# The second feed-forward product by Strassen's scheme, in a transformer layer on one Trainium2 core

## The chip, the cores and the metric

The kernel runs on one core of one Trainium2 chip. The metric is the device time of one execution in microseconds (us); the figure shown for a kernel is the median of several runs. All times below are in us unless another unit stands beside them. Engines: PE is the matrix engine, DVE the vector engine, ACT the scalar engine, POOL the GpSimd engine, and SP the engine on whose queue nearly all DMAs are issued here.

## The reference

One layer of a transformer, with T = 1024 tokens, D = 1024, 16 heads of 64, and a feed-forward width of 2816, in float32:

```
shift1, scale1, gate1, shift2, scale2, gate2 = split(silu(c) @ ada_w + ada_b)
h = x * (1 + scale1) + shift1
y = forgetting_attention(h)                # q, k rms-normed; scores + F_q - F_k, causal softmax; * sigmoid(o); @ w_o
x = layer_norm(ALPHA * x + gate1 * y, ln_g[0], ln_b[0])
h = x * (1 + scale2) + shift2
gate, up = split(h @ ffn_w_in)             # (1024 x 1024) @ (1024 x 5632): the first product
u = silu(gate) * up
out = layer_norm(ALPHA * x + gate2 * (u @ ffn_w_out), ln_g[1], ln_b[1])   # (1024 x 2816) @ (2816 x 1024): the second product
```

Accuracy needs more than one pass of PE: each operand is split into a high and a low part (`hi` is the operand cast to the type fp32r by ACT, `lo` the difference made by DVE), and each product is three matmuls, hi*hi + hi*lo + lo*hi.

## The kernel before, in words

The program is written as Python loops, and a framework puts the instructions of all engines in their final order before the kernel runs; each engine then works through its own list in that order. So the order on an engine can differ from the order of the source, and it is fixed at run time: an instruction that has to wait holds up what stands behind it on its engine or queue.

Stages, with their stretch in the profile: the conditioning and the projections to q, k, v (0 to about 341); the attention (about 341 to 655); the attention's output projection (to about 780); the first feed-forward product (to about 1209); the second, with the last layer norm (to the end).

**Attention.** Head by head. `load` brings a head's operands from DRAM (qa, ka, qb, kb, va). `scores` makes the scores of tiles j = 4, 5, 6, 7, then 0 with 1 and 2 with 3, each in one of two PSUM buffers (`bankS`, tag S, bufs=2), and runs the softmax on each: DVE adds the mask on the diagonal block (L540) and takes the row maximum (L542), ACT exponentiates out of PSUM (L543). A buffer is free again when its exponentials are done. `values` transposes the probabilities on PE (L596), ACT and DVE split them (`ph` L601, `pl` L602), and PE multiplies them with va (L579, L580). `gates` makes the output gate's product (`og`, L631), 24 matmuls for each half of a pair of heads, which can stand anywhere and fill PE. The main loop (L709) takes 12 steps per head, and in each runs a few `og` matmuls, a piece of the next head's scores, and a piece of this head's values. The gate's tanh is followed on POOL by a scaling (L636) and the gate is applied on POOL (L657, L659).

**First product.** Already by Strassen's scheme in Winograd's form: 7 products of half size instead of 8, for 22 blocks of 128 hidden units. `step` runs one product of 12 matmuls into PSUM and combines it on DVE; POOL makes the sums of weights and the product with silu; `prepare` splits the weights eight products ahead. `store_hidden` splits the hidden values (ACT L963, DVE L964) and spills both parts to DRAM (`us`).

**Second product.** Plain: hidden blocks in groups of two (the last has four), eight token tiles, for each 6 matmuls of 512 columns per hidden block (L170 to L172). After each group DVE adds the PSUM tile to a sum in SBUF (L1159). `split_wout` makes ready the weights: POOL multiplies a 128x1024 block by gate2 (L992), ACT casts (L1000), DVE subtracts (L1001). `rest_of_rows` adds the residual rows, three POOL operations of 128x1024 per token tile (L1098 to L1100). With the last group the layer norm of each token tile follows on DVE (L1153, L1154, L1169), its inverse root on POOL (L751).

```
for step in range(12):
    ...
    run(gg, GC[h % 2][step])
    if nxt:
        run(nxt[2])
    run(v)
```

Of the kernel before, what the change touches and what calls it, by code (L numbers as in the profile page):

```python
# [16 lines left out]
P = 128  # L17
# [28 lines left out]
def fox_trunk_kernel(  # L46
# [469 lines left out]

    yp = ctx.enter_context(tc.tile_pool(name="yp", bufs=1, side="right", reuse_waits="tile"))
# [191 lines left out]
    for h in range(H):  # L709
# [3 lines left out]
        for step in range(12):  # L713
            if h % 2 and step in (1, 5):
                hf = HALVES[step == 5]
                state[pr][1][hf] = inverse_sums(pr, hf, state[pr][0][hf])
            if h == H - 1:
                if step == 1:
                    open_h2(HB, hTp, (f"h{HA}", f"l{HA}"))
                    yh, yl = h2h[HB], h2l[HB]  # L720
                if 2 <= step < 2 + NP - 1:
                    split_y(HA, step - 2, yh, yl, nc.gpsimd)
                if step == 6:
                    wo_first = wo_weights(HA, 0, ((ld[0], "owr", 1), (ld[0], "va", 1)))
            run(gg, GC[h % 2][step])
            if nxt:
                run(nxt[2])
            run(v)
# [30 lines left out]
    g2d = dram.tile([1, D], F32, name="g2d")  # L759
    nc.sync.dma_start(g2d, gate2b[0:1, :])  # L760
# [74 lines left out]
    def prepare(n):  # L835
# [11 lines left out]
        if n >= n_first and i == ORDER[-1]:  # L847
            if ff + 2 < NF:
                load_raw(ff + 2)
            else:  # L850
                for m in range(2):
                    load_wraw(ff % 2 * 2 + m)

    wraws = {}

    def load_wraw(ff):
        t = wraws[ff] = ld[0].tile([P, D], F32, name=f"wq{ff}r", tag=RAWS[ff % 4],
                                   **({"bufs": 1} if ff % 4 == 1 else {}))
        nc.sync.dma_start(t, fwo[ff * P:(ff + 1) * P, :])
# [68 lines left out]
    def second_half(k):  # L928
# [9 lines left out]
        hb, hb4 = [fp.tile([P, 512], F32, name=f"hb{n}_{k}", tag=f"hb{n}", bufs=2 - n) for n in range(2)]  # L938
# [3 lines left out]
        t2 = fp.tile([P, 512], F32, name=f"t2_{k}", tag="t2")  # L942
# [17 lines left out]
    def store_hidden(ff, hf, t):  # L960
# [4 lines left out]
        for j, s in enumerate((hi, lo)):  # L965
            move(nc, us[ff][j, :, hf * 512:(hf + 1) * 512], s)


    RING = 6
    rings, parts = {}, {}  # L970

    def load_u(ff):

        r = (ff + 1) % RING
        if r < 4:
            for j in range(2):
                if j not in rings:
                    rings[j] = h2p.tile([P, 4, 2, 512], F32R, name=f"ur{j}", tag="hl"[j])
            t = [rings[j][:, r] for j in range(2)]
        else:  # L980
            if 2 not in rings:
                rings[2] = hTp.tile([P, 2, 2, 2, 512], F32R, name="ur2", tag=f"h{HB}")
            t = [rings[2][:, r - 4, j] for j in range(2)]
        for j in range(2):
            move(nc, t[j].rearrange("p a b -> p (a b)"), us[ff][j])
        parts[ff] = [t, None]

    def split_wout(ff):

        r = (ff + 1) % RING  # L990
        raw = wraws[ff]
        nc.gpsimd.tensor_tensor(raw, raw, gate2b, ALU.mult)  # L992
        if r < 4:
            t = opened[0][:, 2 * r:2 * r + 2]
        else:
            if 3 not in rings:
                rings[3] = Xp.tile([P, 2, 2, 2, 512], F32R, name="wr2", tag="B22")
            t = rings[3][:, r - 4]
        raw2 = raw.rearrange("p (c e) -> p c e", c=2)
        nc.scalar.copy(t[:, :, 0, :], raw2)  # L1000
        nc.vector.tensor_tensor(t[:, :, 1, :], raw2, f32(t[:, :, 0, :]), ALU.subtract)  # L1001
        parts[ff][1] = t

    def ahead(n):
        if n == 0:
            nc.sync.dma_start(gate2b, g2d.to_broadcast([P, D]))
        elif n == 3:
            for ff in range(2):
                load_u(ff)
                split_wout(ff)  # L1010
        elif n == 5:
            load_u(2)
            split_wout(2)

    late = []

    def step(n):
# [30 lines left out]
        elif i == 4:  # L1048
# [3 lines left out]
            late.append(lambda: store_hidden(ff, HA, ua))  # L1052
        else:
# [3 lines left out]
            late.append(lambda: store_hidden(ff, HB, ub))  # L1057
# [31 lines left out]
    accs3 = {hf: hTp.tile([P, 4, D], F32, name=f"out{hf}", tag=f"{t}{HA}") for hf, t in ((HA, "h"), (HB, "l"))}  # L1089
    def out_row(tt):  # L1090
        return accs3[tt // 4][:, tt % 4, :]

    def rest_of_rows(tts):

        for tt in tts:
            t = Xp.tile([P, D], F32, name=f"x1{tt}", tag=f"T{(1, 4)[tt % 2]}")
            nc.sync.dma_start(t, x1d[tt])
            nc.gpsimd.tensor_tensor(t, t, gbs[0], ALU.mult)  # L1098
            nc.gpsimd.tensor_tensor(t, t, gbs[1], ALU.add)
            nc.gpsimd.tensor_tensor(out_row(tt), out_row(tt), t, ALU.add)  # L1100

    groups = [2] * 9 + [4]

    def load_group(n):
        g0 = sum(groups[:n])
        for ff in range(g0, g0 + groups[n]):
            if ff not in parts:
                load_u(ff)
            if ff not in wraws:
                load_wraw(ff)  # L1110
            if parts[ff][1] is None:
                split_wout(ff)

    load_group(1)
    gbs = []
    for n, src in enumerate((ln_g, ln_b)):
        gb = fp.tile([P, D], F32, name=f"gb{n}", tag=f"gb{n}")
        nc.sync.dma_start(gb, src[0, 0:1].to_broadcast([P, D]))
        nc.scalar.mul(gb, gb, ALPHA)
        gbs.append(gb)  # L1120
    tiles = [hf * 4 + o for hf in HALVES for o in range(4)]
    g0 = 0
    for gi, G in enumerate(groups):
        last = gi == len(groups) - 1
        if last:
            lnr = []
            for n, src in enumerate((ln_g, ln_b)):
                t = fp.tile([P, D], F32, name=f"ln2_{n}", tag=f"gb{n}")
                nc.sync.dma_start(t, src[0, 1:2].to_broadcast([P, D]))
                lnr.append(t)  # L1130
        for ti, tt in enumerate(tiles):
            hf, o = divmod(tt, 4)
            end = last and tt == tiles[-1]
            cuts = [(0, 512), (512, 768), (768, 896), (896, 1024)] if end else [(0, 512), (512, 1024)]
            st = fp.tile([P, 4, 6], F32, name=f"st2_{tt}", tag="st2", bufs=2) if last else None
            a = out_row(tt)
            if last and o % 2:
                ys = [ps2.tile([P, 512], F32, name=f"y{g0}_{tt}{cc}", tag="gu"[cc % 2], bufs=2)[:, 0:c1 - c0]
                      for cc, (c0, c1) in enumerate(cuts)]
            else:  # L1140
                y = bankS(f"y{g0}_{tt}").rearrange("p a b -> p (a b)")
                ys = [y[:, c0:c1] for c0, c1 in cuts]
# [65 lines left out]
```

## Time and profile before

| what | value |
|---|---|
| median of 3 runs (lowest, highest) | 1475.2 (1474.42, 1475.4) |
| the profiled execution: its time, its span | 1476.91, 1475.1 |
| busy: PE, DVE, ACT, POOL | 95%, 66%, 38%, 32% of the span |
| mean granted clock of PE | 0.987 of full speed |

PE is busy nearly all the time. A share of 95% is an average over stages: how much a stage leaves idle, and what PE waits for there, has to be read stage by stage. Below, a matmul's duration overlaps the next one's, so the rate of PE is read from the distance between starts.

### The profile page before, as it was taken

To read this page: it belongs to the slowest core of one execution; us is meant where nothing else is said; L and a number is where in the kernel's file an instruction comes from. 1 tells how busy PE (TensorE), PEld (TensorE's weight loads), DVE (VectorE), ACT (ScalarE), POOL (GpSimd) and SP (SyncE) were. 2 spreads that over 40 slices of the span, in tenths; PEclk is the share of its full clock that TensorE was granted. 3 is DMA by queue.
4 is the path that set the end of the run, shared out by engine and by line. 5 is a ranking of instruction groups with operands and counts; after the bars stand their busy time and mean duration, and the time that the engine had idled before them with its cause. 6 is when DMAs were issued, how large, how long until landed. Compare 5 with 4: busy or idle time off the path is not lost.

```text
span 1475.1 us, 19125 instructions
## 1 busy us (share of the span) xinstructions
PE 1396.3 (95%) x6955; PEld 1159.3 (79%) x6955; DVE 968.2 (66%) x1526; ACT 554.0 (38%) x1018; POOL 476.3 (32%) x312
## 2 busy tenths in 40 slices
PE   5899999999999999999998989999999998999997
PEld 4677778877888888889986767888888777777886
DVE  6766576546888888887678655454444554656568
ACT  3432232225777777772445333333333332101000
POOL 2442013300111111140035544444444427784102
PEclk9999999999999999999999999999999999999999
DMA  9757776567656666456363334333333257464212
GB/s 275 198 169 244 231 214 193 172 210 169 142 136 143 146 146 145 116 172 201 128 184 87 129 129 129 105 110 101 114 103 111 101 203 268 143 225 162 73 68 100
DMA packets 194880, 228.45 MB, mean 155 GB/s; under 512 B 11417, under 2 KB 136673, under 8 KB 194786
## 3 DMA queue, kind: packets, MB, share of 16 engines
q1 hardware_dynamic: 193634, 225.13, 50.5%
q10 hardware_dynamic: 1152, 2.10, 0.4%
q8 instruction: 55, 0.90, 0.3%
q14 instruction: 39, 0.32, 0.1%
HBM read 167.88 MB, written 59.31 MB: 154 GB/s over the span
## 4 chain that ended last, share of the span: by engine, by line
PE 63%; DVE 17%; POOL 6%; DMA 5%; issue 4%; ACT 3%; SPq 1%; POOLq 0%; DVEq 0%; ACTq 0%
PE og L631 5%; PE y L170 4%; PE y L171 4%; PE y L172 4%; PE t L596 4%; PE B L1029 3%; PE B L1030 3%; PE B L1031 3%; PE A L1029 3%; PE A L1030 2%; PE A L1031 2%; PE s L535 2%; PE s L536 2%; PE D L1031 2%; PE D L1030 2%
## 5 line engine op out<-in xcount | busy, mean ns | idle before, releaser
L1159 DVE TENSOR_TENSOR out<-y,out 128x1024 f32<-128x1024 f32 x64 | 77.8, 1221 | 79.4 <-PE y L172 77.9
L602 DVE TENSOR_TENSOR pl<-t,ph 128x512 fp32r<-128x512 f32 x192 | 103.7, 548 | 14.9 <-ACT ph L601 13.4
L1029 PE MATMUL B<-XT,slots 128*128 128x512 f32 x264 | 104.2, 395 | 7.0 <-DVE fd L1045 5.3
L543 ACT ACTIVATE p<-s,nm 128x640 f32<-128x640 f32 (+7 forms) x128 | 95.4, 746 | 39.0 <-DVE nm L542 38.6
L601 ACT CAST ph<-t 128x512 fp32r<-128x512 f32 x192 | 90.8, 478 | 44.4 <-PE t L596 42.0
L1030 PE MATMUL B<-XT,slots 128*128 128x512 f32 x264 | 103.1, 390 | 0.0
L1031 PE MATMUL B<-XT,slots 128*128 128x512 f32 x264 | 102.9, 390 | 0.0
L170 PE MATMUL y<-slots,ur 128*128 128x512 f32 (+1 forms) x246 | 96.0, 390 | 6.8 <-DVE out L1159 6.5
L542 DVE TENSOR_REDUCE nm<-s 128x1 f32<-128x640 f32 (+7 forms) x128 | 95.5, 748 | 2.5
L596 PE MATMUL t<-ident,p 128*128 128x128 f32 x576 | 95.6, 274 | 0.6 <-DVE pl L602 0.4
L171 PE MATMUL y<-slots,ur 128*128 128x512 f32 (+1 forms) x246 | 95.3, 387 | 0.0
L172 PE MATMUL y<-slots,ur 128*128 128x512 f32 (+1 forms) x246 | 95.2, 387 | 0.0
L964 DVE TENSOR_TENSOR ul<-fd,uh 128x512 fp32r<-128x512 f32 x44 | 37.5, 851 | 87.8 <-ACT uh L963 87.8
L1029 PE MATMUL A<-h2h,slots 128*128 128x512 f32 x176 | 73.5, 418 | 14.2 <-ACT fc L1039 6.7
L596 PEld LDWEIGHTS t<-ident,p 128*128 128x128 f32 x576 | 71.3, 141 | 11.5 <-DVE pl L602 2.3
L845 ACT CAST slots<-wi 128x512 fp32r<-128x512 f32 x88 | 54.0, 618 | 61.7 <-PE D L1030 35.6
L846 DVE TENSOR_TENSOR slots<-wi,slots 128x512 fp32r<-128x512 f32 x88 | 73.9, 840 | 4.5 <-ACT slots L845 4.1
L579 PE MATMUL o<-ph,va 128*128 128x512 f32 x192 | 76.6, 399 | 0.0
L535 PE MATMUL s<-ka,qa 128*128 128x320 f32 (+2 forms) x192 | 67.5, 352 | 4.8 <-ACT p L543 4.8
L1031 PE MATMUL A<-h2h,slots 128*128 128x512 f32 x176 | 71.3, 405 | 0.0
L1030 PE MATMUL A<-h2l,slots 128*128 128x512 f32 x176 | 71.1, 404 | 0.0
L580 PE MATMUL o<-pl,va 128*128 128x512 f32 x192 | 66.7, 348 | 0.0
(620 smaller groups left out, 3981.2 us busy)
## 6 DMA issues: line engine op xcount, KB each, us to landing
wi<-in_ffn_w_in_dram SPq DMA_DIRECT2D x50, 512.0 KB
aw<-in_ada_w_dram SPq DMA_DIRECT2D x46, 512.0 KB
ur<-us SPq DMA_DIRECT2D x44, 512.0 KB
us<-uh SPq DMA_DIRECT2D x44, 256.0 KB
us<-ul SPq DMA_DIRECT2D x44, 256.0 KB
qa<-qs SPq DMA_DIRECT2D x32, 256.0 KB
vs<-vt SPq DMA_DIRECT2D x16, 512.0 KB
ka<-ks SPq DMA_DIRECT2D x32, 256.0 KB
```

The lines of the kernel that those rows point to most:

```text
L170: nc.tensor.matmul(acc, lh, rh, start=(k == 0), stop=False)
L171: nc.tensor.matmul(acc, lh, rl, start=False, stop=False)
L172: nc.tensor.matmul(acc, ll, rh, start=False, stop=(k == kn - 1))
L535: nc.tensor.matmul(o, qa[:, q], ka[:, c0:c0 + w], start=True, stop=False)
L542: nc.vector.tensor_reduce(nm, view, axis=axis, op=ALU.max, negate=True)
L543: nc.scalar.activation(pv, view, AF.Exp, bias=nm, accum_out=lcs[hf][:, s * 4 + jj:s * 4 + jj + 1])
L596: nc.tensor.transpose(tb[:, jj * P:(jj + 1) * P], probs[hf * 4 + jj][:, kbk * P:(kbk + 1) * P], ident)
L601: nc.scalar.copy(ph[:, c0:], tb[:, c0:])
L602: nc.vector.tensor_tensor(pl[:, c0:], tb[:, c0:], f32(ph[:, c0:]), ALU.subtract)
L1029: nc.tensor.matmul(b, hi, rh, start=(first and k == 0), stop=False, skip_group_check=True)
L1030: nc.tensor.matmul(b, hi, rl, start=False, stop=False, skip_group_check=True)
L1031: nc.tensor.matmul(b, lo, rh, start=False, stop=(k == 3), skip_group_check=True)
```

## The change

The second product becomes Strassen's scheme too: 7 chains over 11 pairs of hidden blocks, each step 4 row tiles x 3 matmuls of 512 columns, the whole chain kept in PSUM: 7 x 11 x 12 = 924 matmuls of 512 columns, where before there were 22 x 8 x 2 x 3 = 1056 (each counted as 512 columns wide). Its operands are sums of quarters of the hidden matrix and of `ffn_w_out`:

- The sums of the weights are made during the attention, one pair of hidden blocks with each of heads 1 to 11 (`out_weights`): two 512 KB loads into the tiles `gate1b` and `gate2b`, four POOL subtractions of 128x512, two 512 KB stores to DRAM (`td`). The two gates themselves are kept in DRAM meanwhile (`gd`) and loaded again later.
- The sums of the hidden values are made by DVE at the end of each pair in the first product, four additions of 128x512 (`hidden_sums`), and stored unsplit; the ACT cast and the DVE subtraction of `store_hidden` are gone.
- The residual rows are scaled in the first product, on DVE (`scaled_row`: two operations of 128x1024 for each of 8 rows), not on POOL in the second.
- In the second product `prep2` splits each of the 77 operand pairs of 128x1024 (ACT, DVE); gate2 is applied to the result on DVE, by a multiplication and an addition of 128x512 per quarter; POOL keeps only the inverse roots.

```diff
+    def out_weights(j, step):
+        b11, b12 = gate1b[:, 0:512], gate1b[:, 512:1024]
+        b21, b22 = gate2b[:, 0:512], gate2b[:, 512:1024]
+        if step == 1:
+            for n, t in enumerate((gate1b, gate2b)):
+                nc.sync.dma_start(t, fwo[(2 * j + n) * P:(2 * j + n + 1) * P, :])
+        elif 4 < step < 9:
+            o, a, b = ((b11, b12, b11), (b12, b22, b12), (b22, b22, b11), (b21, b21, b22))[step - 5]
+            nc.gpsimd.tensor_tensor(o, a, b, ALU.subtract)
+        elif step == 11:
+            for n, t in enumerate((gate1b, gate2b)):
+                nc.sync.dma_start(td[j][:, n].rearrange("p c e -> p (c e)"), t)
...
+            if 1 <= h <= NJ:
+                out_weights(h - 1, step)
...
-        hi = fp.tile([P, 512], F32R, name=f"uh{ff}{hf}", tag="hb0", bufs=2)
-        lo = fp.tile([P, 512], F32R, name=f"ul{ff}{hf}", tag=f"a{hf}")
-        nc.scalar.copy(hi, t)
-        nc.vector.tensor_tensor(lo, t, f32(hi), ALU.subtract)
+    def hidden_sums(ff, ua, ub, va, vb):
...
+        nc.vector.tensor_tensor(s1, ub, vb, ALU.add)
+        nc.vector.tensor_tensor(s2, s1, ua, ALU.subtract)
+        nc.vector.tensor_tensor(ub, ua, ub, ALU.subtract)
+        nc.vector.tensor_tensor(s4, va, s2, ALU.subtract)
...
+        elif i == 7:
+            nc.vector.tensor_tensor(rw[0], rw[0], gate1b, ALU.mult)
+        elif i == 5:
+            nc.vector.tensor_tensor(rw[0], rw[0], gate2b, ALU.add)
...
-        nc.gpsimd.tensor_tensor(raw, raw, gate2b, ALU.mult)
...
+    def prep2(m):
...
+        nc.scalar.copy(t[:, 0], raw)
+        nc.vector.tensor_tensor(t[:, 1], raw, f32(t[:, 0]), ALU.subtract)
...
+    def add_gated(tt, c, t, src):
+        a = rows2[:, tt, c * 512:(c + 1) * 512]
+        todo.append(lambda: nc.vector.tensor_tensor(t, src, gate2b[:, c * 512:(c + 1) * 512], ALU.mult))
+        todo.append(lambda: nc.vector.tensor_tensor(a, a, t, ALU.add))
...
+        if i != ORDER2[-1]:
+            for j in range(NJ):
+                for r in range(4):
+                    products(bs[r], m0 + j, r, 0, 512, NJ)
+                    if j == NJ - 1:
+                        done(i, r, bs[r])
+                if j < NJ - 2:
+                    prep_next(m0 + j + 14, 2)
...
+        for r in range(4):
...
+            for k, (c0, c1) in enumerate(cuts):
+                for j in range(NJ):
+                    products(bs[r], m0 + j, r, c0, c1, NJ)
...
+                if k == 0 and r < 2:
+                    second_rows(2 * r)
+                    second_rows(2 * r + 1)
+                last_rows(r, bs[r], c0, c1, st, k)
```

The framework's final order moves with it, in the attention above all. The first place is PE at the start of head 9's scores. A row gives the source line, the operation, out<-in and the shape; `s9_4` is head 9's score tile 4, `t8` are transposes for the values of head 8, `o7` a values product of head 7, `og4` a gate product. Before, these rows follow one another:

```order
L535 MATMUL s9_4_4927<-ka9_4907,qa9_4906 128x320
L536 MATMUL s9_4_4927<-kb9_4909,qb9_4908 128x320
L596 MATMUL t8_1_0_4931<-ident_58,p8_4_4655 128x128
L596 MATMUL t8_1_0_4931<-ident_58,p8_5_4705 128x128
L596 MATMUL t8_1_0_4931<-ident_58,p8_6_4741 128x128
L596 MATMUL t8_1_0_4931<-ident_58,p8_7_4786 128x128
L579 MATMUL o7_0_4901<-ph7_0_2_4876,va7_4398 128x256
L580 MATMUL o7_0_4901<-pl7_0_2_4877,va7_4398 128x256
L631 MATMUL og4_1_4924<-hTl1_114,woh40_4833 128x512
L535 MATMUL s9_4_4927<-ka9_4907,qa9_4906 128x320
L536 MATMUL s9_4_4927<-kb9_4909,qb9_4908 128x320
```

And of the change, at the same tile (L556 and L557 are the score matmuls there, L617 the transposes, L601 a values product):

```order
L601 MATMUL o8_0_5224<-pl8_0_3_5221,va8_4707 128x128
L557 MATMUL s9_4_4998<-kb9_4980,qb9_4979 128x320
L556 MATMUL s9_4_4998<-ka9_4978,qa9_4977 128x320
L557 MATMUL s9_4_4998<-kb9_4980,qb9_4979 128x320
L557 MATMUL s9_5_5041<-kb9_4980,qb9_4979 128x384
L556 MATMUL s9_5_5041<-ka9_4978,qa9_4977 128x384
L557 MATMUL s9_5_5041<-kb9_4980,qb9_4979 128x384
L556 MATMUL s9_6_5078<-ka9_4978,qa9_4977 128x448
L557 MATMUL s9_6_5078<-kb9_4980,qb9_4979 128x448
L556 MATMUL s9_6_5078<-ka9_4978,qa9_4977 128x448
L557 MATMUL s9_6_5078<-kb9_4980,qb9_4979 128x448
L617 MATMUL t9_1_0_5249<-ident_58,p9_4_4999 128x128
```

The scores of head 9 no longer stand spread among the values of head 8: all values of head 8 stand ahead of them, and between score tiles 6, 7, 0 and 2 stands one transpose of head 9 itself. Heads 5, 7, 11 and 13 look the same. With heads 6, 8, 10 and 12 the scores are bunched likewise, but some rows of the head before and of the gate (2 to 4 of each kind) stand between tiles 5 and 7. Heads 0 to 4, 14 and 15 stand nearly as before, and so do the output projection and the first product.

The second place is SP's queue where the operands of head 8 are loaded. Before:

```order
L42 DMA qa8_4640<-qs4_121 64x1024
L42 DMA ka8_4641<-ks4_129 64x1024
L42 DMA qa8_4640<-qs4_121 64x1024
L42 DMA va7_4398<-vs0_133 128x8x128
L42 DMA ka8_4641<-ks4_129 64x1024
L42 DMA qb8_4642<-qs4_121 64x1024
L42 DMA qb8_4642<-fq_135 4x1024
L42 DMA kb8_4643<-ks4_129 64x1024
```

And of the change (`td5` are the stores of the sums of pair 5, which wait for POOL; `gate1b` and `gate2b` now hold blocks of `ffn_w_out`):

```order
L529 DMA gate2b_107<-in_ffn_w_out_dram 128x1024
L42 DMA qa8_4703<-qs4_121 64x1024
L42 DMA ka8_4704<-ks4_129 64x1024
L535 DMA td5_2783<-gate1b_106 128x1024
L535 DMA td5_2783<-gate2b_107 128x1024
L42 DMA qa8_4703<-qs4_121 64x1024
L42 DMA ka8_4704<-ks4_129 64x1024
L42 DMA qb8_4705<-qs4_121 64x1024
L42 DMA qb8_4705<-fq_135 4x1024
L42 DMA kb8_4706<-ks4_129 64x1024
L42 DMA kb8_4706<-fk_136 4x1024
L42 DMA va8_4707<-vs1_134 128x8x128
```

Most of head 8's operands, qb8 and kb8 among them, now stand behind two stores that wait for four POOL subtractions, which in turn stand on POOL's list behind a gate's scaling.

## Rows read from the trace of the kernel before

**Rows 1.** Busy us and instructions by stretch, PE, PEld, DVE, ACT, POOL; granted clock; DMA.

```profile
1209.00:1300.00 91.00, 82.52 (x348) 66.57 (x347) 48.25 (x32) 20.48 (x22) 65.90 (x26) 0.96 0.57 208
1425.00:1475.00 50.00, 42.27 (x205) 35.60 (x203) 42.01 (x70) 0.00 (x0) 11.37 (x8) 0.93 0.22 85
```

**Rows 2.** PE in time after a stall, start and duration; then the stretch behind it.

```profile
1240.80 0.80 PE L170 MATMUL y<-slots,ur 128*128 128x512 f32 x1 [3.50 <-DVE out L1159]
...
1240.00:1246.50 6.50, 5.70 (x13) 4.46 (x14) 2.05 (x3) 0.00 (x0) 6.42 (x3) 0.50 0.43 158
```

**Rows 3.** Second product by line: busy us, mean ns, idle before; single splits, min/median/max.

```profile
L170 PE MATMUL y<-slots,ur 128*128 128x512 f32 (+1 forms) x246 | 96.0, 390 | 6.8 <-DVE out L1159 6.5 <-ACT out L1157 0.3
L170 PE MATMUL y<-wr,ur 128*128 128x512 f32 (+1 forms) x114 | 44.7, 392 | 5.8 <-DVE out L1159 5.8
...
L1001 DVE TENSOR_TENSOR slots<-wq13r,slots 128x1024 fp32r<-128x1024 f32 x1 | 3.4, 3422 | 0.0
...
L1001 DVE TENSOR_TENSOR wr<-wq3r,wr x1: 1214/1214/1214, 1210.7 to 1210.7; 128x1024 fp32r<-128x1024 f32 x1
```

**Rows 4.** Layer norm at the end by line, and DVE's last row in time.

```profile
L1154 DVE BATCH_NORM_STATS2 st<-out 128x6 f32<-128x512 f32 (+2 forms) x18 | 10.8, 625 | 0.1
L1153 DVE TENSOR_TENSOR out<-y,out 128x512 f32<-128x512 f32 (+2 forms) x18 | 10.7, 615 | 4.2 <-PE y L172 4.2
...
L1169 DVE SCALAR_TENSOR_TENSOR out<-out,mvb,ln 128x1024 f32<-128x1024 f32 (+2 forms) x9 | 10.3, 1157 | 0.0
...
1470.37 1.41 DVE L1169 SCALAR_TENSOR_TENSOR out<-out,rstdb,ln 128x640 f32<-128x640 f32 x2
```

**Rows 5.** PE in time at the end of the first product, and that stretch.

```profile
1165.42 0.39 PE L1029 MATMUL B<-XT,slots 128*128 128x512 f32 x1
...
1167.91 0.39 PE L1031 MATMUL B<-XT,slots 128*128 128x512 f32 x1
1170.83 0.50 PE L1029 MATMUL A<-h2h,slots 128*128 128x512 f32 x1 [2.53 <-ACT fc L1039]
...
1160.00:1209.00 49.00, 44.46 (x181) 35.76 (x180) 24.11 (x26) 13.64 (x22) 19.04 (x11) 0.93 0.45 161
```

**Rows 6.** The first product's long middle, by stretch (columns as in the first group).

```profile
896.00:1160.00 264.00, 262.63 (x1143) 213.17 (x1142) 131.42 (x191) 93.80 (x164) 115.67 (x82) 1.00 0.33 108
```

**Rows 7.** Two heads of the attention, by stretch; the eight stretches that follow repeat them.

```profile
402.00:421.00 19.00, 19.00 (x114) 16.09 (x113) 16.50 (x36) 13.90 (x33) 1.90 (x2) 1.00 0.55 141
421.00:440.00 19.00, 18.43 (x108) 15.80 (x107) 16.25 (x32) 13.27 (x32) 4.45 (x4) 1.00 0.64 141
```

**Rows 8.** PE in time at head 0: first matmul of tiles 4, 6, 7, 0, 2.

```profile
341.17 0.31 PE L535 MATMUL s<-ka,qa 128*128 128x320 f32 x1
...
345.01 0.37 PE L535 MATMUL s<-ka,qa 128*128 128x448 f32 x1
...
345.86 0.48 PE L535 MATMUL s<-ka,qa 128*128 128x512 f32 x1
...
348.77 0.33 PE L535 MATMUL s<-ka,qa 128*128 128x128 f32 x1
...
350.49 0.34 PE L535 MATMUL s<-ka,qa 128*128 128x384 f32 x1
...
351.32 0.39 PE L596 MATMUL t<-ident,p 128*128 128x128 f32 x2
```

**Rows 9.** The softmax on DVE: the mask, 400 to 600; the maximum, whole kernel.

```profile
L540 DVE TENSOR_TENSOR s<-s,maskb 128x128 f32<-128x128 f32 x86 | 25.0, 290 | 13.3 <-PE s L536 9.2 <-ACT p L543 3.2
...
L542 DVE TENSOR_REDUCE nm<-s 128x1 f32<-128x640 f32 (+7 forms) x128 | 95.5, 748 | 2.5
```

**Rows 10.** Attention, 400 to 600, by line: a POOL product, a DVE split.

```profile
L657 POOL TENSOR_TENSOR lb<-lb,sg 128x512 f32<-128x512 f32 x10 | 12.8, 1282 | 45.1 <-DMA lb<-rsd 44.7
...
L615 DVE TENSOR_TENSOR wol<-wor,woh 128x512 fp32r<-128x512 f32 x10 | 11.7, 1168 | 0.8 <-ACT woh L614 0.8
```

**Rows 11.** Waits of SP's queue, 400 to 600: total us, times, longest.

```profile
SPq L42 <- PE t L596: 98.6, 11, 11.9
```

More of the change, by code (lines that the diff above doesn't have):

```diff
@@ L972, in load_u @@
[L972 to L986, printed above, removed]
@@ L988, in split_wout, with store_hidden @@
-    def split_wout(ff):
-        r = (ff + 1) % RING
-        raw = wraws[ff]
-        nc.gpsimd.tensor_tensor(raw, raw, gate2b, ALU.mult)
[L993 to L1002, printed above, removed]
+    def store_hidden(ff, t, i):
+        nc.sync.dma_start(sd[i][ff // 2], t)
@@ L1004, in ahead, with prep_next @@
+    prepped = [0]
+    def prep_next(upto, most):
+        while prepped[0] < min(upto, len(seq2)) and most:
+            prep2(prepped[0])
+            prepped[0] += 1
+            most -= 1
     def ahead(n):
         if n == 0:
[L1006 to L1015, printed above, removed]
+            nc.sync.dma_start(gate2b, gd[1].to_broadcast([P, D]))
+            for m in (4, 5):
+                load_raw2(m)
+        elif n >= 3:
+            prep_next(RING, 1 + n % 2)
@@ L1017, in step @@
+    late, rw = [], [None]
     def step(n):
@@ L1056, in step @@
             nc.gpsimd.tensor_tensor(ub, ub, gb, ALU.mult)
-            late.append(lambda: store_hidden(ff, HB, ub))
+            if ff % 2:
+                late.append(lambda: (store_hidden(ff, ub, 4),
+                                     hidden_sums(ff, fd[:, 4], fd[:, 2], fd[:, 5], fd[:, 3])))
+        if ff == FIRST and i == 6:
+            for t, src in ((gate1b, ln_g), (gate2b, ln_b)):
+                nc.sync.dma_start(t, src[0, 0:1].to_broadcast([P, D]))
+        elif ff == FIRST and i == 3:
+            for t in (gate1b, gate2b):
+                nc.scalar.mul(t, t, ALPHA)
+        elif FIRST < ff <= FIRST + TT:
+            scaled_row(ff - FIRST - 1, i)
         if n + 8 < len(seq):
@@ L1102, in fox_trunk_kernel @@
[L1102 to L1120, printed above, removed]
@@ new lines, in last_rows, with new_st, second_rows @@
+    def last_rows(r, b, c0, c1, st, k):
+        a = rows2[:, HA * 4 + r, 512 + c0:512 + c1]
+        t = tmp[:, r, c0:c1]
+        nc.vector.tensor_tensor(t, b[:, c0:c1], gate2b[:, 512 + c0:512 + c1], ALU.mult)
+        nc.vector.tensor_tensor(a, a, t, ALU.add)
+        nc.vector.bn_stats(st[:, k, :], a)
+    def new_st(tt):
+        return fp.tile([P, 3, 6], F32, name=f"st2_{tt}", tag="st2", bufs=2)
+    def second_rows(r):
+        tt = HB * 4 + r
+        st = new_st(tt)
+        for k in range(2):
+            nc.vector.bn_stats(st[:, k, :], rows2[:, tt, k * 512:(k + 1) * 512])
+        norm2(tt, st[:, 0:2], lnr, ((0, D),))
@@ new lines, in products @@
+    def products(b, m, r, c0, c1, kn):
+        i, j = seq2[m]
+        t = parts[m]
+        rs = slice(r * P, (r + 1) * P)
+        first, last = i in (1, 6, 5) and j == 0, j == kn - 1
+        sh, sl, wh, wl = t[:, 0, 0, rs], t[:, 1, 0, rs], t[:, 0, 1, c0:c1], t[:, 1, 1, c0:c1]
+        nc.tensor.matmul(b[:, c0:c1], sh, wh, start=first, stop=False, skip_group_check=True)
+        nc.tensor.matmul(b[:, c0:c1], sh, wl, start=False, stop=False, skip_group_check=True)
+        nc.tensor.matmul(b[:, c0:c1], sl, wh, start=False, stop=last, skip_group_check=True)
```

198 lines of the change are left out of this document (115 added, 83 removed).

## The prediction

> **What bounds the kernel now.** I read the page's busy shares first, then busy time by stretch, then PE's rows in time at the places where a stretch has a hole, and the waits of SP's queue last. PE bounds nearly everything, so the question for each edit is what PE then waits for.
>
> The second product runs from about 1209 to the end at 1475.1, which is 266.1. PE's rate at full clock is seen where it never waits: from 1165.42 to 1167.91 lie 11 distances between matmuls of 512 columns, 0.2264 each [rows 5]. The plain product has 1056 such matmuls, 239.1 of pure rate. The other 27 are stalls (PE waits 12.3 for DVE's accumulation, L1159, to free a PSUM buffer [rows 3]), stretches at half the clock (0.50 granted for 6.5 after one such stall [rows 2]), and the tail of the last layer norm. Most stalls fall in 1209 to 1300, where POOL is busy 65.90 of 91 [rows 1]: the DVE split of a 128x1024 block takes 1.21 alone and 3.42 when POOL works beside it [rows 3], and the accumulation stands behind it.
>
> The end of the first product has holes too: 1167.91 to 1170.83 is one, and in 1160 to 1209 PE is busy 44.46 of 49 at a clock of 0.93 [rows 5]. Its long middle has none: 262.63 of 264 [rows 6].
>
> The attention repeats every 19.0, PE busy 18.43 to 19.00, DVE 16.25 to 16.50 [rows 7]. Two engines are nearly full there: it runs at PE's pace only because DVE's softmax of the next head lies beside PE's values of this one.
>
> **What the change removes in the second product.** Six chains of 11 steps of 12 matmuls come to 792 x 0.2264 = 179.3. The first operands have to be split at the turn of the stages; I take 2 for that. In these chains DVE has one split (1.21 by the undisturbed row) and up to two gated operations of 0.62 in a step of 2.72, ACT one cast, and POOL nothing, so PE sets the pace. The DMAs bring 77 x 512 KB and 8 MB of rows and output in some 228, about 214 GB/s; the stretch 1209 to 1300 moved 208 at a busy share of 0.57 [rows 1], so that fits.
>
> In the last chain PE has 132 x 0.2264 = 29.9, but DVE has more. Behind the end of the sixth chain it does 9 left-over additions and multiplications of 512 (5.5 at 0.615), 13 statistics of 512 and 2 of 256 (8.7 at 0.625), the last quarters' multiply and add (3 x 2 x 0.615 and 2 x 2 x 0.32: 5.0), and two passes over 8 rows: the 9 pieces of a pass took 9 x 1.157 = 10.4, two passes 20.8 [rows 4]. That is 40.0, and with 16 small operations about 43; as a check, the tail of before, of much the same make, kept DVE busy 42.01 of its last 50 [rows 1]. The final store lies behind it: DVE's last row ends at 1470.37 + 1.41, the span at 1475.1, so 3.3 [rows 4]. Sum: 179.3 + 2 + 46.3 = 227.6 against 266.1: **-38.5**. If PE set the tail, it would be 29.9 + 8 and the gain 47; if operands came late, I bound the loss by the 20 of stalls and clock that this stage has now, a gain of 18.
>
> **The first product.** Its closing holes come from POOL and ACT work for the second product (the gate2 products, casts), which stands ahead of p1's copy. The POOL part goes; eight casts and splits come instead in the last five products of 2.72, on engines with half their time free. The holes cost 4.5 of idle time and 49 x 0.07 = 3.4 of clock, 8 in all; I take **-7** (bounds -8 and 0). `hidden_sums` puts four DVE operations of 512 where four stood, and ACT's casts go; PE hardly waits there [rows 6], so nothing. The scaled rows are 16 DVE operations of 1.2, up to 3.4 beside POOL; DVE is busy 131.42 of 264 there, so they fit, and hurt only when one stands ahead of a PSUM combination that PE needs: I take 0.1 each, **+2** (bounds 0 and +16, at 1.0 each).
>
> **The attention, where work is added.** POOL has 4.45 of 19 at most [rows 7] and gets 4 subtractions at 1.28 [rows 10]: by itself that fits. The two loads and stores bring 2 MB per head to 141 GB/s; that fits too. The cost is in the order: for heads 5 to 13 the scores stand bunched at the turn of the heads. What a bunched head costs shows at head 0, whose scores have no other head to lie beside: tile 4 begins at 341.17, 6 at 345.01, 7 at 345.86, 0 at 348.77, 2 at 350.49, and the next transposes at 351.32 [rows 8]. These 10.15 are set not by PE (it was filled with gate matmuls) but by the two PSUM buffers, each held through mask, maximum and exponentials. A head's scores are 9,216 columns, 4.1 at full rate, 4.4 with the small excess that tile 6 shows (0.85 for 1,792 columns [rows 8]); four transposes add 0.3.
>
> - Heads 5, 7, 9, 11, 13: only these transposes lie between, so PE idles 10.15 - 4.7 = 5.4; minus the start of tiles 4 and 5, issued early, 5.3. Five times: 26.5.
> - Heads 6, 8, 10, 12: 4 gate matmuls, 8 values matmuls and 3 transposes lie between, about 2.4, so 3.4 each: 13.6.
> - The values then run without scores between them, so the chain transpose, ph, pl shows more; I take 0.6 for each of nine heads, 5.4 (bounds 0 and 1.5 each).
> - The clock: a stall of 3.50 was followed by 6.5 at half speed [rows 2], 3.2 lost. I take 4.5 for all nine (bounds 0 and 29).
>
> Since PE is full otherwise, none of it is made up: 26.5 + 13.6 + 5.4 + 4.5 = **+50**.
>
> The Trainium skill (GPSIMD Engine Reference, section 1, Specifications) says that POOL's SBUF interfaces are shared with the vector engine, with contention for DVE instructions in a two-port mode or with two SBUF inputs. By that rule the subtractions disturb only L615 in the attention, which reads two SBUF tiles; mask, maximum and pl read PSUM. The trace agrees as far as it goes: DVE's time is 16.25 in heads where POOL has 4.45 and 16.50 where it has 1.90 [rows 7]. If each L615 (1.17 [rows 10]) were stretched as the split was, to 3.3, that would be 4.3 per pair of heads in DVE's idle time; I add nothing for it.
>
> **Sum.** -38.5 - 7 + 2 + 50 = +6.5, against the profiled execution's 1476.91, 1.7 above the median: 1483.4 there, **1482** as a median, slower by 0.4%.
>
> **The rivals.**
> - *The bunching costs half, and the kernel is faster.* At head 0 DVE waited between tiles. Its own work for eight tiles is 8 x (0.290 + 0.748) = 8.3 [rows 9]; if the scores take only that, the odd heads idle 3.6 and the even ones 1.3, 23.2 in all without clock losses. Then 1475.2 - 43.5 + 23.2 = 1455. Against it: a buffer goes through PE, DVE and ACT in turn, and there are two. It decides where a head loses less than 43.5 / 9 = 4.8.
> - *No loss at all:* 1432. It needs PE to find other work at the turns, and its list holds none.
> - *The next head's operands come late.* qb and kb stand behind stores that wait for POOL, which waits for the gate's tanh. Now the queue waits 9 per head pair for buffers that PE's transposes still hold (98.6 in 11 waits [rows 11]), so loads are ready early and some of that is spare. If 5 per pair are missing, 5.5 pairs cost 27: 1509.
> - *The clock falls at every turn:* nine times 3.2 is 29 in place of 4.5, 1506. The Trainium skill (TensorE: Matmul & The Clock Gate, "A second HAM failure mode") says that a PE which idles briefly between groups while PSUM buffers cycle can swing between its two clock levels. No row here shows such a pattern of short waits; the granted clock at head 0 can't, since PE was full.
> - *The change doesn't save what it says:* late operands in the second product leave a gain of 18 there, 1502.
>
> **How the numbers follow.** The forecast has 0.33, with its own range 1468 to 1497; the faster rival 0.33, no loss 0.06; late operands and falling clock 0.22 together; the starved second product 0.06. The range 1447 to 1509 leaves out the case without loss, and the outer ends of the late and the fast ones. A change of 0.2%, 3 us, is about what a measurement of this kernel tells from none. Faster: 0.30 of the first rival, 0.06, and 0.04 of the forecast, 0.40; within: 0.10; slower: 0.50.
>
> **What would show it.** Attention stretches of two heads: 47 to 50 in place of 38, PE idle in front of score tiles 6, 7, 0 and 2, released by ACT's exponentials (late operands: by a DMA, in front of tile 4). The stage from the first split operand to the end: about 228, with PE ending some 15 before DVE. At the end of the first product, no hole of over 2 ahead of the matmuls that wait for p1's copy. I am wrong if two heads take under 44, or if the second product's chains show waits for the splits.

## The result, and the profile after

The changed kernel takes 1494.82 us (median of 4 runs, 1487.88 to 1499.79), the kernel before 1474.81 beside it: a ratio of 1.0136, 95% interval 1.009 to 1.0182. It is slower, as forecast, and inside the range; the forecast was 1482.

The profiled execution has a span of 1490.4, 15.3 more than before. By the first matmul of each stage in the two traces:

| stage | before | after | difference | forecast |
|---|---|---|---|---|
| attention | 307.1 | 368.4 | +61.3 | +50 |
| output projection | 102.3 | 102.5 | +0.1 | 0 |
| first product | 458.6 | 449.3 | -9.4 | -5 |
| second product | 266.0 | 230.3 | -35.7 | -38.5 |

(What stands ahead of the attention is 1.1 shorter. Before, by these first matmuls, the attention runs from 341.2 to 648.2, its output projection to 750.6 and the first product to 1209.2; the ends at about 655 and 780 given for the first two are too late.) The terms outside the attention came out within 5 of the forecast, and their errors nearly cancel: -45.1 measured, -43.5 forecast. The gap is the attention's.

The page's lines on the engines and on the largest groups, after (columns as in the groups of the second product by line):

```profile
PE 1393.2 (93%) x6832; PEld 1150.2 (77%) x6832; DVE 988.4 (66%) x1572; ACT 590.6 (40%) x1025; POOL 422.7 (28%) x310
...
L1036 DVE TENSOR_TENSOR ring<-r,ring 128x1024 fp32r<-128x1024 f32 x77 | 95.8, 1251 | 62.7 <-ACT ring L1035 58.9
L1221 PE MATMUL y<-ring 128*128 128x512 f32 (+1 forms) x319 | 123.5, 388 | 7.7 <-DVE veb L774 5.5
...
L556 PE MATMUL s<-ka,qa 128*128 128x320 f32 (+2 forms) x192 | 75.9, 405 | 30.2 <-ACT p L564 29.7
```

The splits of the second product now take 1.251 on average, near the shortest of before, 1.214 [rows 3]. In front of the scores PE now idles 30.2, and 29.7 of that ends with ACT's exponentials.

The stretches of the second product after, by engine (columns as in [rows 1]):

```profile
1260.00:1300.00 40.00, 38.22 (x168) 31.00 (x167) 26.11 (x24) 19.30 (x22) 3.69 (x2) 1.00 0.95 342
1380.00:1420.00 40.00, 40.00 (x177) 32.95 (x176) 25.10 (x28) 15.80 (x15) 0.00 (x0) 1.00 0.59 189
1443.00:1490.40 47.40, 33.48 (x166) 28.87 (x165) 39.74 (x68) 0.00 (x0) 11.98 (x8) 0.87 0.23 90
```

PE is idle for 1.8 of the first 40 and then full until 1443, at a clock of 1.00, against 82.52 of 91 and 0.96 at the same place before [rows 1]; the last chain takes 47.4, where 46.3 was forecast. At the end of the first product, where PE stood still for over 2 [rows 5], it is now full:

```profile
1209.00:1260.00 51.00, 51.00 (x226) 41.99 (x225) 27.13 (x37) 18.95 (x27) 11.35 (x8) 1.00 0.46 159
```

Now the attention. First PE in time at head 9's bunched scores (start, duration, what it waited for); compare the tiles of head 0 in [rows 8]:

```profile
488.12 0.34 PE L557 MATMUL s<-kb,qb 68*128 68x384 f32 x1
490.80 0.47 PE L556 MATMUL s<-ka,qa 128*128 128x448 f32 x1 [2.34 <-ACT p L564]
...
493.16 0.63 PE L556 MATMUL s<-ka,qa 128*128 128x512 f32 x1
493.59 0.63 PE L557 MATMUL s<-kb,qb 68*128 68x512 f32 x1
494.02 0.41 PE L617 MATMUL t<-ident,p 128*128 128x128 f32 x1
495.08 0.48 PE L556 MATMUL s<-ka,qa 128*128 128x128 f32 x1 [0.64 <-ACT p L564]
...
497.24 0.69 PE L556 MATMUL s<-ka,qa 128*128 128x384 f32 x1 [0.72 <-ACT p L564]
```

PE waits in front of tiles 6, 0 and 2, each time for the exponentials that free a score buffer. From 493.16 the matmuls of 512 columns start 0.43 apart, not 0.23: the clock has fallen. The pair of heads from there, by stretches of equal clock:

```profile
488.00:491.26 3.26, 0.92 (x5) 0.59 (x4) 2.88 (x5) 1.09 (x3) 3.02 (x4) 1.00 0.19 78
491.26:501.50 10.24, 8.87 (x28) 6.46 (x27) 6.49 (x15) 5.16 (x13) 1.23 (x1) 0.50 0.89 221
501.50:521.98 20.48, 17.65 (x99) 14.21 (x98) 14.04 (x27) 12.14 (x27) 6.09 (x6) 1.00 0.42 135
521.98:525.39 3.41, 3.41 (x14) 2.68 (x13) 3.38 (x5) 1.75 (x5) 3.33 (x3) 0.50 0.95 282
525.39:539.30 13.91, 13.91 (x82) 11.63 (x81) 8.29 (x17) 8.01 (x18) 3.52 (x4) 1.00 0.99 238
sum 51.30, PE 44.76 PEld 35.57 DVE 35.08 ACT 28.14 POOL 17.20; mean PE 8.95 PEld 7.11 DVE 7.02 ACT 5.63 POOL 3.44
```

Two heads take 51.3 where they took 38.0 [rows 7]. PE is idle for 51.3 - 44.8 = 6.5 of it, 0.6 before: 6.0 more. And PE works 8.87 + 3.41 = 12.3 at half clock, which costs half of that, 6.1. So waits and clock have equal parts; 1.2 of the 13.3 is left over. The whole attention, after and then before:

```profile
340.00:708.00 368.00, 334.68 (x1742) 268.85 (x1741) 271.81 (x528) 226.75 (x519) 114.47 (x95) 0.93 0.67 177
...
341.00:648.00 307.00, 301.58 (x1745) 254.48 (x1743) 261.85 (x528) 221.29 (x519) 57.30 (x52) 1.00 0.57 136
```

PE is idle for 33.3 after and 5.4 before, 27.9 more. The clock was 0.50, the lower of its two levels (1.2 and 2.4 GHz), for 54.6 of it after, never before; PE worked in 50.4 of these 54.6, which costs 25.2. Of the 61.3, 8.2 is left over, and no run here says where it goes.

What SP's queue waited for in the attention, 400 to 660 (total, times, longest):

```profile
SPq L535 <- POOL gate1b L532: 69.9, 9, 11.1
SPq L669 <- DVE rr L668: 28.2, 8, 11.7
SPq L535 <- DMA gate1b<-in_ffn_w_out_dram: 16.3, 4, 5.8
SPq L535 <- POOL gate2b L532: 14.0, 9, 2.3
```

Before, the queue's waits were mostly for buffers of the next heads [rows 11], that is, it was ahead. Now it stands 9 times at a store of sums, up to 11.1, for POOL. Yet PE in the changed kernel never waits for an operand's load: the framework put the scores late enough on PE's list.

### The profile page after: what moved, and what is told of

Its sections match the earlier page's. It is cut to its first block, busy times and chain, and to the rows that moved or that the text cites. A ratio compares the mean times of both kernels' runs of the same rounds, so it can differ in the third digit from the quotient of the medians.

```text
span 1490.4 us, 19190 instructions
## 1 busy us (share of the span) xinstructions
PE 1393.2 (93%) x6832; PEld 1150.2 (77%) x6832; DVE 988.4 (66%) x1572; ACT 590.6 (40%) x1025; POOL 422.7 (28%) x310
## 5 line engine op out<-in xcount | busy, mean ns | idle before, releaser
L1036 DVE TENSOR_TENSOR ring<-r,ring 128x1024 fp32r<-128x1024 f32 x77 | 95.8, 1251 | 62.7 <-ACT ring L1035 58.9
L1221 PE MATMUL y<-ring 128*128 128x512 f32 (+1 forms) x319 | 123.5, 388 | 7.7 <-DVE veb L774 5.5
L1222 PE MATMUL y<-ring 128*128 128x512 f32 (+1 forms) x319 | 122.9, 385 | 0.0
L1035 ACT CAST ring<-r 128x1024 fp32r<-128x1024 f32 x77 | 80.4, 1056 | 107.1 <-DMA r<-td 35.1
L1223 PE MATMUL y<-ring 128*128 128x512 f32 (+1 forms) x319 | 122.7, 385 | 0.0
L617 PE MATMUL t<-ident,p 128*128 128x128 f32 x576 | 105.8, 288 | 1.3 <-DVE pl L623 1.1
L556 PE MATMUL s<-ka,qa 128*128 128x320 f32 (+2 forms) x192 | 75.9, 405 | 30.2 <-ACT p L564 29.7
L617 PEld LDWEIGHTS t<-ident,p 128*128 128x128 f32 x576 | 77.7, 149 | 26.5 <-DVE pl L623 7.4
L1071 PE MATMUL A<-h2h,slots 128*128 128x512 f32 x176 | 70.8, 402 | 8.2 <-ACT fc L1083 3.2
L1221 PEld LDWEIGHTS y<-ring 128*128 128x128 f32 x319 | 61.1, 192 | 22.3 <-DVE veb L774 6.1
L556 PEld LDWEIGHTS s<-ka,qa 128*128 128x128 f32 x192 | 39.2, 204 | 48.5 <-ACT p L564 44.6
L557 PE MATMUL s<-kb,qb 68*128 68x320 f32 (+2 forms) x192 | 70.6, 380 | 0.0
```

The costliest lines, as they stand in the source:

```text
L556: nc.tensor.matmul(o, qa[:, q], ka[:, c0:c0 + w], start=True, stop=False)
L617: nc.tensor.transpose(tb[:, jj * P:(jj + 1) * P], probs[hf * 4 + jj][:, kbk * P:(kbk + 1) * P], ident)
L1036: nc.vector.tensor_tensor(t[:, 1], raw, f32(t[:, 0]), ALU.subtract)
L1071: nc.tensor.matmul(b, hi, rh, start=(first and k == 0), stop=False, skip_group_check=True)
L1221: nc.tensor.matmul(b[:, c0:c1], sh, wh, start=first, stop=False, skip_group_check=True)
L1222: nc.tensor.matmul(b[:, c0:c1], sh, wl, start=False, stop=False, skip_group_check=True)
```

## The experiments

The theory after this profile: the change's own work costs little; the loss is the order on PE, which follows from SP's queue, and half of it comes through the clock. The rivals are: the added POOL work or traffic costs wherever it stands; or the loss comes from elsewhere in the change.

**Without the sums.** The attention as before; the second product loads weight blocks in place of the sums, so its result is another one.

```diff
-            if 1 <= h <= NJ:
-                out_weights(h - 1, step)
-            elif h == NJ + 2 and step == 1:
+            if h == NJ + 2 and step == 1:
...
-            nc.sync.dma_start(t[:, 1], td[j][:, i in (4, 6), i in (6, 7)])
+            r0, c0 = (2 * j + (i in (4, 6))) * P, (i in (6, 7)) * 512
+            nc.sync.dma_start(t[:, 1], fwo[r0:r0 + P, c0:c0 + 512])
```

> The changed kernel without the sums of the weights in the attention (no loads, subtractions or stores there); the second product loads blocks of the weights themselves in their place, of the same size, so the output is not the reference's. PE's list in the attention is again that of before. Theory (the sums' place in the attention costs what the attention lost): the attention takes 307 again instead of 368, the rest stays, so 1494.8 - 61 = about 1434, 2.8% faster than before. Rival (the loss comes partly from elsewhere, for example from gates kept in DRAM or from the stages after): over 1445.

Measured: 1433.83 (ratio to before 0.9699, interval 0.9666 to 0.9731), attention 307.0. Two heads at full speed, in one stretch of 38:

```profile
500.00:538.00 38.00, 37.42 (x220) 31.90 (x219) 32.75 (x67) 27.14 (x66) 6.39 (x7) 1.00 0.61 141
```

So everything but the sums is worth 42.6 (before took 1476.44 on the same chip), and making the sums in the attention costs 61. The rival that the loss comes from elsewhere falls.

**Loads and stores on POOL's queue.** All the work of the change; PE's order is that of before.

```diff
-                nc.sync.dma_start(t, fwo[(2 * j + n) * P:(2 * j + n + 1) * P, :])
+                nc.gpsimd.dma_start(t, fwo[(2 * j + n) * P:(2 * j + n + 1) * P, :])
...
-                nc.sync.dma_start(td[j][:, n].rearrange("p c e -> p (c e)"), t)
+                nc.gpsimd.dma_start(td[j][:, n].rearrange("p c e -> p (c e)"), t)
```

> The changed kernel with all its work, but the two loads and the two stores of the sums issued on POOL's queue instead of SP's, so that the next head's operands no longer stand behind them; the order of scores and values on PE is then that of before in all heads. Theory (the order costs the time, not the added work): attention 307 to 311, total 1434 to 1438. Rival (POOL's subtractions and 22 MB of traffic disturb the attention themselves): the attention stays over 335, total over 1460.

Measured: 1497.83 (ratio to before 1.0144, interval 1.0115 to 1.0173), attention 367.3. A miss: the order is that of before, and the time is lost all the same. What PE waited for in the attention of this kernel, and then POOL, ACT and SP:

```profile
PE s L556 <- ACT p L564: 27.9, 8, 15.5
PE s L556 <- DMA ka<-ks: 10.7, 1, 10.7
PE s L557 <- DMA kb<-fk: 9.9, 2, 8.6
PE s L557 <- DMA kb<-ks: 6.2, 2, 3.9
...
POOL gate1b L532 <- DMA gate2b<-in_ffn_w_out_dram: 33.1, 10, 7.1
POOL gate1b L532 <- DMA gate1b<-in_ffn_w_out_dram: 20.7, 10, 4.5
POOL gate2b L529 <- DMA td<-gate2b: 16.9, 8, 4.6
POOL gate1b L529 <- DMA td<-gate1b: 16.1, 8, 3.8
...
ACT sg L656 <- POOL lb L678: 24.8, 2, 15.4
...
SPq L749 <- DMA td<-gate1b: 23.5, 1, 23.5
SPq L673 <- POOL y L680: 17.8, 4, 6.4
```

About half of this is the rival of late operands. POOL's list is in order: the loads wait there for the stores ahead of them, the subtractions for the loads, and behind these stands the gate's work. So two things come late. SP's queue stands for a buffer that the gate still reads (L673), and once for 23.5 at the reload of `gate1b`, behind the last store of sums (L749); the next head's ka and kb, behind these, keep PE waiting up to 10.7. And ACT stands twice, 24.8 in all, at the gate's tanh (L656), whose buffer POOL's product (L678) has not yet read; the exponentials stand behind it on ACT's list, so PE's longest wait, 15.5 until 475.85, ends with an exponential that came late, though one takes only about 1. Freeing one queue has moved the coupling to others.

**The bunching alone.** No sums at all; the loop gives a head's scores after the values of the head before.

```diff
             run(gg, GC[h % 2][step])
-            if nxt:
-                run(nxt[2])
             run(v)
+        if nxt:
+            run(nxt[2], 12)
```

> As the kernel without the sums, but the loop gives each head's scores after all values of the head before; 11 or 27 other matmuls (gate and transposes) then stand between a head's scores from the second tile on, against 3 or 15 in the changed kernel and 54 or 58 before. No added POOL work, no added traffic. Output not the reference's for the same reason. Theory (bunched scores wait for the two PSUM buffers, and the clock falls at those waits): the attention takes some 340 to 375 for 15 heads, PE waits for ACT's exponentials ahead of scores for 25 or more. Rival (the loss needs the late operands or the POOL work): attention 307 to 312.

Measured: 1492.78 (one run), attention 362.4, 55 over the kernel without the sums, which is the same but for the bunching. The attention in one stretch:

```profile
340.00:703.00 363.00, 331.99 (x1748) 264.93 (x1746) 266.60 (x528) 227.22 (x519) 58.50 (x52) 0.94 0.47 116
```

and PE's largest wait in it (total, times, longest):

```profile
PE s L556 <- ACT p L564: 28.6, 29, 1.8
```

Without one added transfer or POOL operation an order like this makes nearly the same loss with the same marks: waits for exponentials of 28.6 (29.7 in the changed kernel) and a clock of 0.94 (0.93). It is not the changed kernel's order, though: here 13 heads, 2 to 14, are bunched, with 11 or 27 other matmuls between their scores, there nine, with 3 to 16. So this shows that bunching by itself can cost as much; how much of the 61 it makes is not measured by it.

**The kernel before with the sums.** The function `out_weights`, its DRAM tiles and its calls added to the kernel before, results not used.

> The kernel before with the sums of the weights made in its attention as in the change, their results not used; everything else as before. Theory (the attention's loss is independent of the rest of the change): attention 368, total 1475 + 61 = 1536. Rival (another part of the change, such as the new stages' buffers or order, takes part): attention under 350 or total under 1520.

Measured: 1531.2 (one run), attention 368.4: the attention's loss is independent of the rest of the change. The whole is 55 longer than before, not 61; some stages outside the attention came out a few shorter.

**The sums in the projections.** All the work, but `out_weights` runs through the projections, with the tiles that later hold qa, ka, qb and kb.

```diff
+            ts = [ld[0].tile([P, D], F32, name=f"ow{n}_{j}", tag=(("qa", "ka"), ("qb", "kb"))[j % 2][n]) for n in range(2)]
...
             for f in later.pop(0, []):
                 f()
+            next(sums_gen, None)
```

> The changed kernel with all its work, the sums of the weights made in the projections instead of the attention (loads and stores on SP's queue, subtractions on POOL, with the tiles that later hold the heads' operands). Scores and values on PE are spread again from head 4 on, nearly so from head 2. Theory (the sums cost only where SP's queue and PE have no slack): attention 307 to 312, projections up to 10 longer, total 1434 to 1446. Rival (22 MB of traffic and 44 POOL operations cost some 60 wherever they stand): total over 1465.

Measured: 1474.21 (ratio to before 0.9985, interval 0.9963 to 1.0006). A miss, on the rival's side of 1465: the sums cost 40 here (1433.83 without them), where 10 at most was expected and the rival had 60. The loss is in the projections: their last matmul begins at 378.2 (340.9 before), and the output projection at 686.4, 38 later than before. One of the projections to v, for instance, took 71.0 (58.4 before), the DMAs busy 0.83 of it (0.71 before):

```profile
142.60:213.60 71.00, 57.85 (x246) 43.74 (x244) 47.66 (x58) 19.02 (x26) 18.15 (x13) 0.93 0.83 269
```

In the projections PE waited for DVE's sums, which wait for loads, and SP for POOL:

```profile
PE arp L445 <- DVE ar L436: 10.3, 3, 7.0
PE arp L449 <- DVE ar L436: 9.4, 2, 5.8
...
SPq L510 <- POOL ow L507: 41.0, 15, 7.6
```

So the coupling is there again: the stores wait 41.0 for POOL on the queue that brings the weights. What the fuller DMAs cost beside it is not separated here.

**Half of the work each.** Subtractions only (no loads, no stores), and loads and stores only (no subtractions); the second product gets blocks of the same size, with another result.

> The changed kernel with the POOL subtractions in the attention, but without their loads and stores; the second product loads blocks of the weights of the same size in place of the sums, so the output is not the reference's. The order of scores and values on PE is that of before. Theory (the wait for POOL on SP's queue costs, not the subtractions): attention 307 to 310, total about 1434. Rival (POOL's two-input operations slow DVE's softmax): attention over 320.

> The changed kernel with the loads and stores in the attention, but without the four subtractions between them, so the stored blocks are the weights themselves and the output is not the reference's. On PE 10 to 43 other matmuls stand between a head's scores from the second tile on, between the changed kernel's 3 to 16 and the 54 to 58 of before. Theory (bunching costs by its degree): attention 325 to 350, total 1450 to 1475. Rival (without the wait for POOL nothing is lost): attention under 315.

Measured, one run each: subtractions only 1441.88, attention 307.4; loads and stores only 1463.51, attention 330.3 at a clock of 0.98. POOL's 44 operations cost the attention nothing. The loads and stores alone cost 23, with an order half as bunched; the attention in one stretch:

```profile
345.00:675.00 330.00, 315.00 (x1743) 257.26 (x1742) 261.31 (x528) 224.57 (x519) 58.81 (x52) 0.98 0.66 169
```

How much of the 23 is the order's and how much the traffic's, this run does not tell. The two together cost 61. I put the other 38 down to the store that has to wait for POOL and bunches the order further; no run changes that wait alone.

**Filling the waits.** Matmuls that nobody reads, behind score tiles 5, 6 and (in the same way, not shown) 0 of heads 5 to 13.

```diff
+            if 5 <= h <= 13 and j in (5, 6):
+                for _ in range(20 if j == 5 else 24):
+                    nc.tensor.matmul(st[:, 0, w:512], qa[:, 0:P], ka[:, w:512], start=True, stop=True,
+                                     skip_group_check=True)
```

> The changed kernel with matmuls whose result nobody reads, added for heads 5 to 13 behind score tiles 5, 6 and 0 (20 of 128 columns, 24 of 64, 5 of 384: some 3 at full clock per head), where PE waits for a score buffer. Theory (21 of the attention's loss is the fallen clock, which follows from PE's waits): the granted clock in the attention rises, half-speed stretches under 30 in place of 54.6, and the attention takes 345 to 365 in spite of 27 of added matmuls. Rival (the waits alone cost, or the clock does not follow them): clock as before and attention 368 to 395.

Measured: 1490.15 (one run), attention 364.9. The clock returns, the time hardly moves, and the numbers lie where they were expected; but not for the reason expected. The attention in one stretch:

```profile
341.00:706.00 365.00, 358.11 (x2187) 308.94 (x2186) 264.24 (x528) 224.36 (x520) 115.06 (x96) 0.99 0.66 179
```

the added matmuls by line:

```profile
L576 PE MATMUL s<-ka,qa 128*128 128x64 f32 (+1 forms) x396 | 46.0, 273 | 0.0
L590 PE MATMUL s<-ka,qa 128*128 128x384 f32 x45 | 9.4, 338 | 0.0
```

and what is left of the wait:

```profile
PE s L556 <- ACT p L564: 4.7, 10, 1.1
```

The added matmuls took 55, twice what I had reckoned, and with them the framework's order changed: in this trace 54 or 58 other matmuls, the added ones not counted, stand between the scores of each of the heads 8 to 15 from the second tile on, as many as before the change, and 44 for head 7. The scores lie spread again, which leaves hardly any waits without added matmuls too (before, and without the sums), so the run tells neither whether filled waits bring the clock back nor what the fallen clock costs. It is a test of the order instead: all the work of the sums is there, on SP's queue and on POOL, and 364.9 less the 55 is some 310, 3 more than before. (The added matmuls also lengthen each head, which gives the queue and POOL more time.)

**The sums in the first product.** All the work; one pair with each of hidden blocks 11 to 21, the subtractions on DVE, the residual rows scaled in blocks 7 to 10 so that `gate1b` and `gate2b` are free. Then the same with the last product in one cut, and with the subtractions on POOL.

```diff
-        elif FIRST < ff <= FIRST + TT:
-            scaled_row(ff - FIRST - 1, i)
+        elif FIRST < ff <= FIRST + TT:
+            scaled_row(ff, i)
+        if 11 <= ff < 11 + NJ:
+            out_weights(ff - 11, i)
...
-            cuts = ((0, 256), (256, 512)) if r == 3 else ((0, 512),)
+            cuts = ((0, 512),)
```

> The changed kernel with all its work, the sums of the weights made in the first product instead of the attention, one pair with each of hidden blocks 11 to 21, the four subtractions on DVE; the residual rows are scaled in blocks 7 to 10 instead of 7 to 14, so that their tiles are free for it. The attention's order is that of before. Theory (the sums cost nothing where SP's queue, DMA and DVE have slack: DMA share 0.33 and DVE half busy there): attention 307, first product 449 to 458, total 1434 to 1443. Rival (22 MB of traffic cost 30 to 60 wherever they stand, as in attention and projections): total over 1460.

> As the kernel with the sums in the first product, and the last product of the second stage in one cut of 512 columns instead of two of 256: PE no longer waits for DVE between the cuts (4.36 in the changed kernel, with half speed behind it). Theory (that wait ends last): 3 to 6 less than with two cuts, 1429 to 1439. Rival (DVE's norm work ends last, and the larger last piece makes its tail longer): the same or up to 2 more.

> As the kernel with the sums in the first product, the subtractions on POOL. Theory (POOL's two-input operations stretch DVE's splits beside them): the first product 3 to 15 longer than with DVE. Rival (they fit on either engine): the same within 3.

Measured: 1455.12 with two cuts (ratio to before 0.9862, interval 0.9828 to 0.9895), 1450.28 with one (0.9829, 0.9799 to 0.9859), 1470.39 on POOL (one run). The first two beat both kernels, by less than expected: the sums aren't free here either. In the first, the attention is 307.1 again, but the first product takes 470.3, 21 more than in the changed kernel. DVE's subtractions in the middle of it, 1010 to 1180, by line:

```profile
L1004 DVE TENSOR_TENSOR gate1b<-gate2b,gate1b 128x512 f32<-128x512 f32 x9 | 8.0, 886 | 12.1 <-DMA gate2b<-in_ffn_w_out_dram 12.1
L1004 DVE TENSOR_TENSOR gate1b<-gate1b 128x512 f32<-128x512 f32 x9 | 7.9, 873 | 12.7 <-DMA gate1b<-in_ffn_w_out_dram 12.7
```

and PE's waits there:

```profile
PE D L1071 <- DVE fd L1089: 6.0, 3, 2.2
PE B L1071 <- DVE fd L1085: 5.9, 5, 2.2
```

The subtractions stand on DVE's list until their load has landed, and the combinations that PE needs stand behind them. On POOL the first product takes 17 more still, over the 15 expected at most. There the subtractions and their wait stand ahead of POOL's product for the hidden values; DVE stands at the sums of these (`hidden_sums`), and the combinations that PE needs behind it:

```profile
DVE hs L985 <- POOL fd L1098: 37.0, 4, 14.2
...
PE B L1071 <- DVE fd L1085: 22.4, 4, 8.2
```

The one cut ended the last stage 2.5 earlier: PE's wait for DVE between the cuts, 5.5 in all, fell to 1.4.

## Why the prediction was right, and where its size was off

**The decider was right.** The order of the attention decides against the saving of the second product. Bunching alone, without any of the change's work, makes the same waits, a fallen clock and a loss of 55, though in more heads and less tightly; with all the work and the scores spread again, the attention loses some 3 beside the added matmuls; POOL's part alone loses nothing.

**The term that was off is the attention's, +50 for +61.3, and that it came so near is partly luck.** Of its parts the idle time was forecast at 45.5 (26.5 + 13.6 + 5.4) and measured 27.9; the clock was forecast at 4.5 and measured 25.2; 8.2 is left over. Two errors of 18 and 21 in opposite directions nearly cancel. For the two heads shown, 9.9 of idle time and 1.0 of clock were forecast, 6.0 and 6.1 measured. The idle time was too high, as I read the rows, because while the clock is low the scores themselves fill more of it, and because PE's wait at tile 7 is nil. The clock was sized by one fall of before, behind a wait of 3.50 [rows 2], and taken to be rare. But another stall of before already showed a fall behind a shorter wait: behind the wait of 2.53 in [rows 5] the clock was 0.50 from 1171.40 to 1174.81. In the attention it falls behind waits of 2.34, and the half speed that follows lasts 10.24 at three of the turns. The rival "the clock falls at every turn" had the mechanism and, with 29, nearly the price; what I missed is that it doesn't stand beside the waits as an alternative, it comes together with them. The Trainium skill's remark (TensorE: Matmul & The Clock Gate, "A second HAM failure mode"), that short waits while PSUM buffers cycle can make the clock swing, agrees with the granted clock of 0.50 at 491.26 and 521.98.

**The second product**: 230.3 for 227.6. Six chains took 183 for 181. (The split taken as undisturbed, 1.214 [rows 3], had POOL at work beside it for 0.39; two with none in the same trace took 1.224 and 1.225, so the term stands. Another with POOL beside it for 0.99 took 1.216, so not all of POOL's work stretched a split.) The last took 47.4 for 46.3, but DVE, busy 39.74 of it, was not the only cause. PE in time at the second cut of the last tile, its last matmul, and DVE's last row:

```profile
1475.74 0.58 PE L1221 MATMUL y<-ring 128*128 128x256 f32 x1 [4.08 <-DVE veb L774]
...
1482.03 0.28 PE L1223 MATMUL y<-ring 128*128 128x256 f32 x1
...
1485.39 1.41 DVE L1170 SCALAR_TENSOR_TENSOR rows<-rows,rstdb,ln 128x640 f32<-128x640 f32 x2
```

PE waited 4.08 for DVE there and then ran at half speed, so it ended 4.5 ahead of DVE, not 15. The experiment with one cut shows that this was worth 2.5.

**The first product**: -9.4 for -5. The holes at its end are gone entirely; that end is 8 shorter. The scaled rows cost more than the 2 that I took: from 956 to 1050, where they stand, PE waited 4.1 for DVE's combinations. That is made up by the rest of the middle, where a matmul took 0.226 on average (159 for 704, from 1050 to 1209) and 0.231 before (264 for 1143 [rows 6]); I hadn't forecast this, and its cause stays open.

**The contention of POOL and DVE**: subtractions alone left the attention at 307.4, so adding nothing for it was right.

**Late operands** were a rival with its own price; in the changed kernel they don't occur. In the experiment with POOL's queue they make about half of PE's waits, beside an ACT held up by POOL, at the same loss.

## What to carry to other kernels

Work put on an idle engine isn't free if its result leaves through a queue that others need: ask what stands behind the store that waits for it, on every list that it passes. Compare the order on the bound engine before and after, and price a bunched stretch by the chain through its PSUM buffers, plus the half speed that came with such waits here. Then look for the stage whose queue has slack: the same sums cost 61 in the attention, about 40 in the projections and about 20 in the first product, where the change does pay.

## What the runs showed of the hardware that I had not expected

The clock fell to 0.50 at 491.26 behind one wait of 2.34, in a stretch in which PE had otherwise been busy, and stayed there for 10.24 while PE was busy 8.87 of it; at 521.98 it fell behind waits of 1.00 and 1.76. With the bunching alone it fell too (0.94 over the attention), though no wait there was longer than 1.8. Matmuls of 64 and 128 columns with one and the same stationary operand started 0.11 apart in the experiment with the added matmuls (20 of 128 in 2.2, 24 of 64 in 2.6), no faster for fewer columns, where those of 512 columns start 0.23 apart; so narrow fillers are dear.
